# Queries and keys of an mLSTM layer projected token-major ahead of the values, and turned to features through VectorE and DRAM

## The chip, the cores and the metric

The program runs on one core of one Trainium2 chip. The metric is the device time of one execution in microseconds (us); for a kernel that was run several times it is the median of the runs. Beside the runs there is one execution taken by the hardware profiler, from which the page and the trace come; its span is counted from the first to the last instruction of the core.

The engines are named as in the profile: PE is TensorE with its matmuls, PEld its weight loads, DVE is VectorE, ACT is ScalarE, POOL is GpSimd and SP is SyncE, which here only issues DMAs. Each engine takes its instructions in a fixed order.

## The reference

The model is a decoder trunk of two layers over 256 tokens of width 2048, all in float32. The even layer joins a gated linear recurrence and a real-gated recurrent unit; the odd layer, which the change touches, is an mLSTM with eight heads (key width 128, value width 256) and an output gate. Each layer ends with a gated per-layer embedding. Cut to the odd layer:

```
hn = rmsnorm(h, o_norm)
u  = hn @ o_w_in            # 2048 -> 2048 (q,k) + 2048 (v) + 2048 (og) + 2048 (z) + 16 (gates)
qk = silu(causal_conv(u[qk], c_conv_w, c_conv_b))     # 4 taps along the tokens
li, lf = ig + c_b_i, log_sigmoid(fg + c_b_f)
yc = mlstm(q, k, v, li, lf)                            # stabilised, causal
yc = head_rmsnorm(yc, c_norm) * sigmoid(og) * silu(z)
h  = h + yc @ o_w_out
h  = h + sigmoid(h @ ple_gate_w) * rmsnorm(p @ ple_w, ple_norm)
```

The convolution runs along the tokens, for each of the 2048 query and key features by itself; the scores of the mLSTM need queries and keys with features on the partitions.

## The kernel before

**Products in three parts.** Every large product is made from float32 operands that are each split into a high part (`fp32r`) and a rest: high times high, high times rest, rest times high. `load_weights` (lines 119 to 134) does it for the weights: SP loads half a megabyte into a `raw` tile (line 128; five buffers), ACT casts it to `whi` (line 131) and DVE subtracts to get `wlo` (line 132); of `whi` and of `wlo` there are four buffers each, so a fifth tile can be cast only when PE has finished with the first. The activations are split the same way into tiles `ahl`.

**Two ways to project.** Token-major (`project_tok`, `quarter_tok`, lines 190 to 229): the activations are the stationary operand and the weights stream through, 512 columns at a time; one chunk of 512 output features takes four quarters of 24 matmuls (12 for the first 128 tokens, then 12 for the others), and the result has tokens on the partitions. Feature-major (`block`, lines 154 to 169): the weights are stationary and the activations stream; 128 output features take 16 matmuls of 512 columns (line 161: high weights with high and rest of the activations side by side) and 16 of 256 columns (line 167: rest of the weights), and the result has features on the partitions. `project` (line 176) joins two such blocks: ACT copies one half out (line 173), DVE adds the halves (line 174) and multiplies by the row norm (line 184). `chunks` (line 209) begins a stage with two chunks whose quarters are interleaved (line 203), since the activations of the last quarter arrive late.

**Lanes.** Longer side work is written as generators in named lanes (`start`, `step`, `drain`). `pump` (line 74) takes one step of each lane; it is called in the middle of each token-major quarter (line 229) and in the middle of each feature-major block (line 164). What a step issues is put behind the matmuls already recorded. The order of the instructions on each engine is then fixed by a scheduler that knows these orders, priorities and buffers.

**Turning tokens to features.** `to_features` and `feature_major` (lines 377 and 515) do it in three parts: DVE transposes the 32x32 squares of a 128x1024 tile into `w` (lines 382, 520); `across` (line 504) lets POOL write `w` to a DRAM tensor (line 507) and read it back with the squares in their new places into `r` (four DMAs, line 510); some pumps later ACT brings `r` into order while it applies a gain (lines 390, 527). `w` and `r` share four buffers (`room`, line 905). The kernel does this with the residual ahead of each gate product and with three quarters of the mLSTM's result.

**The odd layer.** Its stages on PE follow each other in this order: gate product of the even layer's embedding (`ple_gate`, line 932); values, token-major (line 970); queries and keys, feature-major, as 16 blocks in pairs (`qk_proj`, line 951): per pair of blocks ACT and DVE also run the convolution (line 958, then three taps per 128 features, line 961) and SiLU (tanh on ACT, line 964, and line 965 on DVE); output gate (line 1093) and gate z (line 1106), both token-major; the output product; the last gate product. The lane `mix` runs beside them: `gate_stats` (line 990) the input and forget gates, then `mix(j)` (line 1027) for two heads each: the stabilising weights (lines 265, 1034 to 1040), two pumps later the scores (lines 1047 to 1049), one pump later scores times values (lines 1059 to 1066). `mix(j)` is started when the queries and keys of its two heads are there. Tiles with the tag `vt` (six buffers) hold values, numerators and gates.

Of the kernel before, what the change touches and what calls it, by code (L numbers as in the profile page):

```python
# [11 lines left out]
F32 = mybir.dt.float32  # L12
# [3 lines left out]
AF = mybir.ActivationFunctionType  # L16
ALU = mybir.AluOpType
PSUM = bass.MemoryType.PSUM

P = 128  # L20
T = 256
# [22 lines left out]
def trunk(ctx: ExitStack, tc: tile.TileContext, a, out):  # L44
    nc = tc.nc
    v, s, gp, te, sy = nc.vector, nc.scalar, nc.gpsimd, nc.tensor, nc.sync
# [16 lines left out]
    def start(lane, gen):  # L63
        lanes.setdefault(lane, []).append(gen)
# [16 lines left out]
    def drain(*which):  # L81
        for lane in which:
            while step(lane):
                pass
# [26 lines left out]
    def pc(name, i=0, n=None):  # L111
        o, w = PRM[name]
        return prm[:, o + i:o + i + (n or 1)]
# [62 lines left out]
    def project(w, pair, act, which=(0, 1), rs=None):  # L176

        m = tp.tile([P, 512], F32, name="mg", tag="hn", bufs=3)
        for j in which:
            merge(m[:, j * T:(j + 1) * T], block(w[2 * pair + j], act))  # L180
        if rs is not None:
            n = len(which)
            m3 = m[:, which[0] * T:(which[0] + n) * T].rearrange("p (j t) -> p j t", j=n)
            v.tensor_tensor(out=m3, in0=m3, in1=rs.unsqueeze(1).to_broadcast([P, n, T]), op=ALU.mult)
        return m
# [275 lines left out]
    acth = []  # L461
# [28 lines left out]
    norm = {}  # L490
# [457 lines left out]
    with tc.tile_pool(name="m1", bufs=2) as m1:  # L948
        qk = {}

        def qk_proj(j):
            ps = project(a["oqk"], j, acth, rs=norm["rs"])
            d = m1.tile([P, 512], F32, name="qk", tag="qk", bufs=8)
            for i in range(2):
                b = 2 * j + i
                dst = d[:, i * T:(i + 1) * T]
                pi = ps[:, i * T:(i + 1) * T]
                s.activation(dst, pi, AF.Identity, scale=pc("ccw", 48 + b), bias=pc("ccb", b))  # L958
                for k in range(2, -1, -1):
                    sh = 3 - k  # L960
                    v.scalar_tensor_tensor(dst[:, sh:T], pi[:, 0:T - sh], pc("ccw", k * 16 + b), dst[:, sh:T],  # L961
                                           op0=ALU.mult, op1=ALU.add)
            th = tp.tile([P, 512], F32, name="th", tag="th")
            s.activation(th, d, AF.Tanh, scale=0.5)
            v.scalar_tensor_tensor(d, th, 1.0, d, op0=ALU.add, op1=ALU.mult)
            return d

        VW = 257
        vts = []
        for j, psv in enumerate(chunks(a["ov"], 4, acth, ready(acth, "fg"))):  # L970
            if j == 0:
                drain("norm")
            vt = m1.tile([P, 2, 2, VW], F32, name="vt", tag="vt", bufs=6)
            gp.memset(vt[:, :, :, 256:VW], 1.0)
            for hf in range(2):
                s.activation(vt[:, hf, :, 0:256], psv[hf].rearrange("p (i e) -> p i e", i=2), AF.Copy,
                             scale=norm["rt"][:, hf:hf + 1])
            vts.append(vt)
        gm = tp.tile([P, T], F32, name="sm", tag="sm")
        s.copy(gm, gps[:, 0:T])  # L980

# [88 lines left out]
        def mix_norm():  # L1070


            t, r, yh = (m1.tile([P, 16], F32, name=n, bufs=1) for n in ("nwt", "nwr", "nwy"))
            s.activation(den, den, AF.Abs)
            v.tensor_tensor(out=den, in0=den, in1=aT[:, 16:32], op=ALU.max)
            v.tensor_scalar(den, den, 1e21, EPS ** 0.5, op0=ALU.min, op1=ALU.mult)
            v.tensor_tensor(out=den, in0=den, in1=den, op=ALU.mult)
            v.scalar_tensor_tensor(den, ss, 1.0 / 256, den, op0=ALU.mult, op1=ALU.add)
            newton(den, t, r, yh)
            for hf in range(2):  # L1080
                c = slice(hf * 8, hf * 8 + 8)
                v.tensor_scalar(fac[:, c], r[:, c], norm["rt"][:, hf:hf + 1], 0.25, op0=ALU.mult, op1=ALU.mult)
            yield

        y = {}
        for j in range(4):
            qk[j] = qk_proj(j)
            qk[4 + j] = qk_proj(4 + j)
            start("mix", mix(j))
        start("mix", mix_norm())  # L1090
        held = []
        for j in range(4):
            ps = project_tok(a["oog"], j, acth)
# [179 lines left out]
def layout(x, p, e_norm, e_w_in, a_lb_logits, a_norm, b_conv_w, b_conv_b, b_w_r, b_b_r, b_w_i, b_b_i, b_lambda,  # L1273
# [4 lines left out]
    def put(name, arr):  # L1278
# [34 lines left out]
        "ez": _tm(za),  # L1313
        "bw": np.ascontiguousarray(bw.transpose(0, 3, 1, 2, 4).reshape(2, P, 2, 512)),
        "eo": _tm(wo),
        "oqk": _fm(ow[:, 0:2048]),
        "ov": _tm(ow[:, 2048:4096]),
        "oog": _tm(ow[:, 4096:6144]),
        "oz": _tm(ow[:, 6144:8192]),
# [23 lines left out]
```

## Time and profile before

| | |
|---|---|
| median of 3 runs | 1051.92 us (1051.46 to 1054.58) |
| profiled execution | 1052.27 us, its span 1050.2 us |
| granted TensorE clock | 0.998 |
| PE busy | 1040.0 us, 99% of the span |
| DVE, ACT, POOL busy | 729.0, 588.9, 105.5 us |
| last two value chunks | 527.5 to 571.1 us |
| queries and keys | 571.1 to 675.5 us |
| output gate, gate z | 675.5 to 762.8, 762.8 to 854.2 us |

The profiled execution is 0.35 us above the median of the runs, and 2.1 us longer than its span. In the trace a row of a timeline has the start, the length, the engine, the line and operation, the tiles as output<-input, their shape, and a count where equal rows are merged; the idle time of the engine just before it stands in brackets with what ended it. Matmuls overlap: one of 512 columns is shown with 0.39 us, but the next begins 0.23 us after it. So PE's work is read from starts, not from lengths.

### The profile page before, as it was taken

The numbers are of one execution on the slowest core, as the hardware profiler recorded it, in microseconds if no ns is written. First come the engines' busy times: TensorE is split into PE (matmuls) and PEld (weight loads), VectorE is DVE, ScalarE is ACT, GpSimd is POOL, SyncE is SP. The second block draws the span as 40 slices with busy tenths as digits, with TensorE's granted clock in tenths as the row PEclk, the third lists the DMA queues.
The fourth block names the chain that finished last, engine by engine and source line by source line (L and its number), as shares of the span: only waits on it lengthen the run. The fifth ranks groups of instructions, "written<-read, shape, count | busy, mean of one in ns | idle before, by whom it ended". The sixth has DMA issues, their size and how long they took to land.

```text
span 1050.2 us, 15196 instructions
## 1 busy us (share of the span) xinstructions
PE 1040.0 (99%) x5632; PEld 876.2 (83%) x5632; DVE 729.0 (69%) x1101; ACT 588.9 (56%) x885; POOL 105.5 (10%) x142
## 2 busy tenths in 40 slices
PE   9999999999999999999999999999999999999996
PEld 7888888888888888887888888888888888888886
DVE  6856897997877666766544887764457777666675
ACT  7775545869654444565544656654445565444553
POOL 0001332522201111111000000000001110111000
PEclk9999999999999999999999999999999999999999
DMA  9865454545867887687556544545557785877652
GB/s 356 302 209 196 166 168 155 181 156 194 273 234 247 264 242 235 207 276 225 188 191 200 173 154 156 170 161 197 197 189 222 249 269 185 291 244 241 201 181 81
DMA packets 63242, 221.21 MB, mean 211 GB/s; under 512 B 7744, under 2 KB 9024, under 8 KB 63168
## 3 DMA queue, kind: packets, MB, share of 16 engines
q1 hardware_dynamic: 55440, 196.38, 56.0%
q0 software_dynamic: 7152, 23.07, 7.2%
q8 instruction: 44, 0.72, 0.3%
q10 hardware_dynamic: 576, 0.79, 0.2%
q14 instruction: 30, 0.25, 0.1%
HBM read 209.20 MB, written 11.01 MB: 210 GB/s over the span
## 4 chain that ended last, share of the span: by engine, by line
PE 98%; DMA 1%; ACT 0%; SPq 0%; DVE 0%; issue 0%; ACTq 0%
PE mm L225 20%; PE mm L227 19%; PE mm L226 19%; PE mm L161 17%; PE mm L167 9%; PE mx L225 2%; PE mx L227 2%; PE mx L226 2%; PE mm L338 2%; PE mm L1178 1%; PE mm L1177 1%; PE mm L1176 1%; DMA raw<-in_pw_dram 1%; PE mx L823 1%; PE nu L1059 1%; PE mx L661 0%
## 5 line engine op out<-in xcount | busy, mean ns | idle before, releaser
L132 DVE TENSOR_TENSOR wlo<-raw,whi 128x1024 fp32r<-128x1024 f32 (+1 forms) x364 | 438.0, 1219 | 241.9 <-ACT whi L131 203.1
L131 ACT CAST whi<-raw 128x1024 fp32r<-128x1024 f32 (+1 forms) x364 | 378.0, 1042 | 354.8 <-PE mm L227 238.3
L225 PE MATMUL mm<-whi,ahl 128*128 128x512 f32 x896 | 350.3, 391 | 0.0
L227 PE MATMUL mm<-whi,ahl 128*128 128x512 f32 x896 | 348.6, 389 | 0.0
L226 PE MATMUL mm<-wlo,ahl 128*128 128x512 f32 x896 | 348.5, 389 | 0.0
L225 PEld LDWEIGHTS mm<-whi,ahl 128*128 128x128 f32 x896 | 168.2, 188 | 36.4 <-issue 1.6
L227 PEld LDWEIGHTS mm<-whi,ahl 128*128 128x128 f32 x896 | 168.2, 188 | 35.3
L226 PEld LDWEIGHTS mm<-wlo,ahl 128*128 128x128 f32 x896 | 168.2, 188 | 34.7 <-DVE wlo L132 0.2
L161 PE MATMUL mm<-ahl,whi 128*128 128x512 f32 x768 | 183.1, 390 | 0.0
L161 PEld LDWEIGHTS mm<-ahl,whi 128*128 128x128 f32 x768 | 141.3, 188 | 27.5
L167 PE MATMUL mm<-ahl,wlo 128*128 128x256 f32 x768 | 102.1, 286 | 0.0
L167 PEld LDWEIGHTS mm<-ahl,wlo 128*128 128x128 f32 x768 | 97.2, 191 | 3.6 <-issue 0.4
L225 PE MATMUL mx<-whi,ahl 128*128 128x512 f32 x96 | 37.5, 391 | 0.0
L227 PE MATMUL mx<-whi,ahl 128*128 128x512 f32 x96 | 37.4, 389 | 0.0
L226 PE MATMUL mx<-wlo,ahl 128*128 128x512 f32 x96 | 37.3, 389 | 0.0
L173 ACT COPY sm<-mm 128x256 f32<-128x256 f32 x48 | 17.6, 367 | 32.1 <-PE mm L167 31.9
L507 POOL DMA_DIRECT2D ducn<-w x3 | 1.7, 563 | 332.5 <-DVE w L520 332.5
L961 DVE SCALAR_TENSOR_TENSOR qk<-mg,prm,qk 128x255 f32<-128x255 f32 (+2 forms) x48 | 21.1, 477 | 5.0 <-ACT qk L958 4.7
L227 PEld LDWEIGHTS mx<-whi,ahl 128*128 128x128 f32 x96 | 18.0, 188 | 3.8
L226 PEld LDWEIGHTS mx<-wlo,ahl 128*128 128x128 f32 x96 | 18.0, 188 | 3.7
L225 PEld LDWEIGHTS mx<-whi,ahl 128*128 128x128 f32 x96 | 18.0, 188 | 3.7
L174 DVE TENSOR_TENSOR mg<-mm,sm 128x256 f32<-128x256 f32 x48 | 19.9, 415 | 0.1
(299 smaller groups left out, 862.1 us busy)
## 6 DMA issues: line engine op xcount, KB each, us to landing
raw<-in_ew_dram SPq DMA_DIRECT2D x64, 512.0 KB, 4.4
raw<-in_g_dram SPq DMA_DIRECT2D x56, 512.0 KB, 4.7
raw<-in_eo_dram SPq DMA_DIRECT2D x32, 512.0 KB, 5.0
raw<-in_ov_dram SPq DMA_DIRECT2D x32, 512.0 KB, 4.1
raw<-in_oqk_dram SPq DMA_DIRECT2D x32, 512.0 KB, 4.3
raw<-in_oog_dram SPq DMA_DIRECT2D x32, 512.0 KB, 3.9
raw<-in_oz_dram SPq DMA_DIRECT2D x32, 512.0 KB, 4.3
raw<-in_oo_dram SPq DMA_DIRECT2D x32, 512.0 KB, 4.5
```

Of the source, the lines that this page charges most:

```text
L131: last["act"] = s.copy(h, r).ins
L132: last["dve"] = v.tensor_tensor(out=l, in0=r, in1=h.bitcast(F32), op=ALU.subtract).ins
L161: last["pe"] = te.matmul(ps, parts[k // 8][0][:, c:c + P], act[k // 2][2][:, (k % 2) * 512:(k % 2 + 1) * 512], start=(k == 0), stop=False).ins
L167: last["pe"] = te.matmul(ps[:, T:2 * T], parts[k // 8][1][:, c:c + P], act[k // 2][0][:, k % 2], start=False, stop=(k == KT - 1)).ins
L173: s.copy(small, ps[:, T:2 * T])
L174: v.tensor_tensor(out=dst, in0=ps[:, 0:T], in1=small, op=ALU.add)
L225: te.matmul(ps[hf], xh, wh, start=(k == 0), stop=False)
L226: te.matmul(ps[hf], xh, wl, start=False, stop=False)
L227: last["pe"] = te.matmul(ps[hf], xl, wh, start=False, stop=(k == KT - 1)).ins
L338: last["pe"] = te.matmul(ps[hf], tokens(pact[x], k, hf), (hi, lo)[y][:, k * 512:(k + 1) * 512], start=(n == mine[0]), stop=(n == mine[-1]) ...
L823: te.matmul(ps[:, i * T:(i + 1) * T], bw[:, w, c * P:(c + 1) * P], xc[:, c * T:(c + 1) * T], start=True, stop=True)
L961: v.scalar_tensor_tensor(dst[:, sh:T], pi[:, 0:T - sh], pc("ccw", k * 16 + b), dst[:, sh:T], op0=ALU.mult, op1=ALU.add)
```

## The change

The weights of queries and keys are laid out for token-major products, and their stage is moved ahead of the values. It starts with the two interleaved chunks, as the values did. Each of its four chunks (512 features, tokens on the partitions) is copied out of PSUM by ACT with the row norm as its scale, into a tile `tqk` with the tag `vt`. A lane per chunk, `features`, transposes the squares, sends them through DRAM with the same `across` and its six pumps of delay, and then, for each pair of 128 features, lets ACT put the squares in order (a plain copy), and runs convolution and SiLU as before. The values follow as four plain chunks; after value chunk j the lanes of the features that heads 2j and 2j+1 need are drained and `mix(j)` is started. The feature-major blocks of this stage, their copies, sums and products with the norm are gone. Nothing else is edited.

```diff
-        def qk_proj(j):
-            ps = project(a["oqk"], j, acth, rs=norm["rs"])
-            d = m1.tile([P, 512], F32, name="qk", tag="qk", bufs=8)
...
+        def features(t, j):
+
+            w = room("w")
+            w5 = w.rearrange("p (j c h t) -> p h c j t", j=4, c=4, h=2)
+            for hf in range(2):
+                v.transpose(w5[:, hf], t[:, hf].rearrange("p (c j q) -> p c j q", c=4, j=4))
+            r = room("r")
+            yield from across(w, r, f"dqk{j}", 6)
+            r5 = r.rearrange("p (i c h t) -> p c h i t", i=4, c=4, h=2)
+            for b in range(2):
+                x = tp.tile([P, 512], F32, name="xr", tag="hn", bufs=3)
+                d = m1.tile([P, 512], F32, name="qk", tag="qk", bufs=8)
+                for i in range(2):
+                    n = 4 * j + 2 * b + i
+                    dst = d[:, i * T:(i + 1) * T]
+                    pi = x[:, i * T:(i + 1) * T]
+                    s.copy(pi.rearrange("p (h i t) -> p h i t", h=2, i=4), r5[:, 2 * b + i])
+                    s.activation(dst, pi, AF.Identity, scale=pc("ccw", 48 + n), bias=pc("ccb", n))
+                    for k in range(2, -1, -1):
+                        sh = 3 - k
+                        v.scalar_tensor_tensor(dst[:, sh:T], pi[:, 0:T - sh], pc("ccw", k * 16 + n), dst[:, sh:T],
+                                               op0=ALU.mult, op1=ALU.add)
+                th = tp.tile([P, 512], F32, name="th", tag="th")
+                s.activation(th, d, AF.Tanh, scale=0.5)
+                v.scalar_tensor_tensor(d, th, 1.0, d, op0=ALU.add, op1=ALU.mult)
+                qk[2 * j + b] = d
+                yield
+
+        for j, ps in enumerate(chunks(a["oqk"], 4, acth, ready(acth, "fg"))):
+            if j == 0:
+                drain("norm")
+            t = m1.tile([P, 2, 512], F32, name="tqk", tag="vt", bufs=6)
+            for hf in range(2):
+                s.activation(t[:, hf], ps[hf], AF.Copy, scale=norm["rt"][:, hf:hf + 1])
+            start(f"qk{j}", features(t, j))
+            step(f"qk{j}")
...
-        for j, psv in enumerate(chunks(a["ov"], 4, acth, ready(acth, "fg"))):
...
         for j in range(4):
-            qk[j] = qk_proj(j)
-            qk[4 + j] = qk_proj(4 + j)
+            psv = project_tok(a["ov"], j, acth)
+            vt = m1.tile([P, 2, 2, VW], F32, name="vt", tag="vt", bufs=6)
+            gp.memset(vt[:, :, :, 256:VW], 1.0)
+            for hf in range(2):
+                s.activation(vt[:, hf, :, 0:256], psv[hf].rearrange("p (i e) -> p i e", i=2), AF.Copy,
+                             scale=norm["rt"][:, hf:hf + 1])
+            vts.append(vt)
+            for c in (j // 2, 2 + j // 2):
+                drain(f"qk{c}")
             start("mix", mix(j))
...
-        "oqk": _fm(ow[:, 0:2048]),
+        "oqk": _tm(ow[:, 0:2048]),
```

**PE, at the scores of two heads.** In the kernel before, the four matmuls of the scores of `mix(1)` stand between the two halves of a feature-major block:

```order
L161 MATMUL mm<-ahl,whi 128x512 x16
L1047 MATMUL mx<-qk 128x256
L1048 MATMUL mx<-qk 128x128
L1047 MATMUL mx<-qk 128x256
L1048 MATMUL mx<-qk 128x128
L167 MATMUL mm<-ahl,wlo 128x256 x16
```

After the change the scores (now lines 1058 and 1059) stand in the middle of a token-major quarter of the values, first those of `mix(0)` in the third quarter of the second value chunk:

```order
L226 MATMUL mm<-wlo,ahl 128x512
L227 MATMUL mm<-whi,ahl 128x512
L1058 MATMUL mx<-qk 128x256
L1059 MATMUL mx<-qk 128x128
L1058 MATMUL mx<-qk 128x256
L1059 MATMUL mx<-qk 128x128
L225 MATMUL mm<-whi,ahl 128x512
```

What moved: rows of lines 161 and 167 no longer stand in this stage, and the side matmuls, the same in number, are set into rows of lines 225 to 227.

**DVE, where convolutions stand between the splits of weights.** Before, in the stage of queries and keys (`mg` is the joined pair of blocks, `sm` the half that ACT copied, `scw` the weighted scores):

```order
L174 TENSOR_TENSOR mg<-mm,sm 128x256
L965 SCALAR_TENSOR_TENSOR qk<-th,qk 128x512
L132 TENSOR_TENSOR wlo<-raw,whi 128x1024 x2
L174 TENSOR_TENSOR mg<-mm,sm 128x256
L184 TENSOR_TENSOR mg<-mg,hrs 128x512
L961 SCALAR_TENSOR_TENSOR qk<-mg,prm,qk 128x255
L961 SCALAR_TENSOR_TENSOR qk<-mg,prm,qk 128x254
L961 SCALAR_TENSOR_TENSOR qk<-mg,prm,qk 128x255
```

After it, in the fourth chunk of queries and keys, from the second split for its second quarter on (`xr` is a pair of feature tiles brought back from DRAM):

```order
L132 TENSOR_TENSOR wlo<-raw,whi 128x1024
L956 STREAM_TRANSPOSE w<-tqk 128x4x4x32
L971 SCALAR_TENSOR_TENSOR qk<-xr,prm,qk 128x255 x2
L971 SCALAR_TENSOR_TENSOR qk<-xr,prm,qk 128x254 x2
L971 SCALAR_TENSOR_TENSOR qk<-xr,prm,qk 128x253 x2
L132 TENSOR_TENSOR wlo<-raw,whi 128x1024 x2
L975 SCALAR_TENSOR_TENSOR qk<-th,qk 128x512
L971 SCALAR_TENSOR_TENSOR qk<-xr,prm,qk 128x255 x2
L971 SCALAR_TENSOR_TENSOR qk<-xr,prm,qk 128x254 x2
L971 SCALAR_TENSOR_TENSOR qk<-xr,prm,qk 128x253 x2
L132 TENSOR_TENSOR wlo<-raw,whi 128x1024 x2
L975 SCALAR_TENSOR_TENSOR qk<-th,qk 128x512
```

What moved: the sums of line 174 and products of line 184 are gone, transposes of line 956 have come, and the taps of the first two chunks, which end a quarter apart, now stand in one run, six before every two splits of weights.

More of the change, by code (lines that the diff above doesn't have):

```diff
@@ L949, in trunk @@
         qk = {}
-        def qk_proj(j):
-            ps = project(a["oqk"], j, acth, rs=norm["rs"])
-            d = m1.tile([P, 512], F32, name="qk", tag="qk", bufs=8)
[L954 to L966, printed above, removed]
+        def features(t, j):
[24 more added lines that the diff above has]
+                yield
@@ L968, in trunk @@
+        for j, ps in enumerate(chunks(a["oqk"], 4, acth, ready(acth, "fg"))):
[6 more added lines that the diff above has]
+            step(f"qk{j}")
         VW = 257
         vts = []
-        for j, psv in enumerate(chunks(a["ov"], 4, acth, ready(acth, "fg"))):
[L971 to L978, printed above, removed]
@@ L1083, in mix_norm @@
             yield
-        y = {}
         for j in range(4):
-            qk[j] = qk_proj(j)
-            qk[4 + j] = qk_proj(4 + j)
+            psv = project_tok(a["ov"], j, acth)
[7 more added lines that the diff above has]
+                drain(f"qk{c}")
             start("mix", mix(j))
         start("mix", mix_norm())
+        y = {}
         held = []
```

## The prediction

> **What bounds the kernel now.** I read the page's busy times first, then the table of waits for PE.
>
> ```profile
> PE 1040.0 (99%) x5632; PEld 876.2 (83%) x5632; DVE 729.0 (69%) x1101; ACT 588.9 (56%) x885; POOL 105.5 (10%) x142
> ```
> ```profile
> PE st L95 <- POOL ones L90: 1.1, 1, 1.1
> PE mm L338 <- DVE wlo L132: 0.4, 1, 0.4
> ```
>
> PE is busy for 99% of the span, and the whole table of its waits (us in total, times, longest) holds two rows, 1.5 us, both at the start. So the kernel is a queue of matmuls, and a change is worth what it takes off that queue, less the waits that it brings. Waits could come from DVE and ACT, which split each weight tile. A table by stage shows their load: the gate product with the first two value chunks; the last two value chunks; queries and keys. Its columns are the stretch and its length, busy time of PE, PEld, DVE, ACT and POOL, the granted clock, the DMA share and GB/s.
>
> ```profile
> 418.00:527.50 109.50, 109.50 (x502) 88.33 (x502) 70.25 (x95) 62.71 (x92) 11.20 (x24) 1.00 0.72 227
> 527.50:571.10 43.60, 43.60 (x194) 36.09 (x193) 19.67 (x17) 19.43 (x20) 0.00 (x0) 1.00 0.58 193
> 571.10:675.50 104.40, 104.40 (x590) 90.84 (x589) 81.89 (x141) 66.04 (x121) 0.00 (x0) 1.00 0.51 167
> ```
>
> DVE has 0.78 of the query-and-key stage and 0.45 of the value chunks ahead of it. The clock is granted in full throughout, so durations can be carried from one stage to another.
>
> **Part 1: 16 feature-major blocks become four token-major chunks.** The chain shows a block as 16 matmuls of line 161 and 16 of line 167; PE's timeline in the value stage shows the starts of two matmuls that are 96, one chunk, apart.
>
> ```profile
> 583.13 3.65 PE mm L161 x16
> 586.78 1.91 PE mm L167 x16
> 588.69 3.65 PE mm L161 x16
> ```
> ```profile
> 527.59 0.39 PE L225 MATMUL mm<-whi,ahl 128*128 128x512 f32 x1
> ...
> 549.35 0.39 PE L225 MATMUL mm<-whi,ahl 128*128 128x512 f32 x1
> ```
>
> A block lasts 588.69 - 583.13 = 5.56 us, 16 of them 88.96 us. A chunk lasts 549.35 - 527.59 = 21.76 us (0.2267 per matmul), four of them 87.04 us. The difference is **-1.92 us**. It comes from the 256-column matmuls: 1.91/16 = 0.119 us each, more than half of the 0.228 of a 512-column one.
>
> The Trainium skill ("TensorE: Matmul & The Clock Gate", section "Back-to-back issue gap") states 518 cycles for 512 columns and 262 for 256 at 2.4 GHz; by these figures a block would be an estimated 5.20 us, a chunk 20.72, and the gain 0.3 us. The rows are 5% and 9% above the page's figures, and they decide.
>
> **Part 2: the side matmuls are set into another stream.** Their number is the same. One whole `mix` in feature-major surroundings lies in four blocks of the chain; one in token-major surroundings lies in the eight chunks of the output gate and gate z.
>
> ```profile
> 622.05 3.65 PE mm L161 x16
> ...
> 648.84 3.65 PE mm L161 x16
> ```
> ```profile
> 675.48 0.40 PE L225 MATMUL mm<-whi,ahl 128*128 128x512 f32 x1
> ...
> 854.25 0.39 PE L338 MATMUL mm<-whi,ahl 128*128 128x512 f32 x1
> ```
>
> The first costs 26.79 - 4 x 5.56 = 4.55 us, the second 178.77 - 8 x 21.76 = 4.69. Three `mix` change surroundings (the fourth had token-major ones already): 3 x 0.14 = **+0.4 us**. The gate sums (lines 993 and 1017) change too and have no row in token-major surroundings; I take 0 for them, since the scores' restarts cost alike in both. From below the term is 0, from above I double it: +0.8.
>
> **Part 3: DVE and ACT.** By the rows of single operations (busy, mean ns, then idle time before), of DVE in the query-and-key stage and of ACT in the odd layer's first half:
>
> ```profile
> L132 DVE TENSOR_TENSOR wlo<-raw,whi 128x1024 fp32r<-128x1024 f32 x32 | 37.8, 1220 | 6.7 <-ACT whi L131 2.9 <-issue 2.8 <-PE mm L167 0.8
> L961 DVE SCALAR_TENSOR_TENSOR qk<-mg,prm,qk 128x254 f32<-128x254 f32 x14 | 6.6, 480 | 0.2
> ...
> L174 DVE TENSOR_TENSOR mg<-mm,sm 128x256 f32<-128x256 f32 x15 | 6.2, 417 | 0.1
> L184 DVE TENSOR_TENSOR mg<-mg,hrs 128x512 f32<-128x512 f32 x7 | 4.8, 692 | 0.2
> L965 DVE SCALAR_TENSOR_TENSOR qk<-th,qk 128x512 f32<-128x512 f32 x7 | 4.8, 689 | 1.3 <-ACT th L964 1.3
> ```
> ```profile
> L390 ACT ACTIVATE xr<-r,prm 128x256 f32<-128x256 f32 x16 | 7.2, 501 | 0.0
> ...
> L173 ACT COPY sm<-mm 128x256 f32<-128x256 f32 x16 | 5.9, 366 | 13.0 <-PE mm L167 13.0
> ...
> L964 ACT ACTIVATE th<-qk 128x512 f32<-128x512 f32 x8 | 5.0, 626 | 3.1 <-DVE qk L961 3.1
> ```
> ```profile
> 436.06 0.70 DVE L382 STREAM_TRANSPOSE w<-hq 128x512 f32<-128x512 f32 x1
> 436.69 0.71 DVE L434 SCALAR_TENSOR_TENSOR hq<-th,rp,hq 128x512 f32<-128x512 f32 x1
> 437.32 2.35 DVE L132 TENSOR_TENSOR wlo<-raw,whi 128x1024 fp32r<-128x1024 f32 x2
> ```
>
> DVE loses 16 sums and 8 products, 6.7 + 5.5 = 12.2 us, and gains 8 transposes of 0.70, 5.6. ACT loses 16 copies, 5.9 us, and gains 16 copies of `xr` (the trace has no plain copy of this view: between 0.37 as line 173 and 0.50 as line 390, which reads the same view; I take 0.50) and 8 copies of 512 columns (about 0.63 as line 964): +7.1 us net. DVE then has 95 of these 148 us, 0.64. What matters is one crowd: chunks 1 and 2 of the stage end one quarter apart, and the taps and SiLU rows of both fall into the four quarters of the fourth chunk, as the rows in the part on the change show. How early a split is done, the value stage shows:
>
> ```profile
> 532.95 2.59 DVE L132 TENSOR_TENSOR wlo<-raw,whi 128x1024 fp32r<-128x1024 f32 x2 [2.85 <-ACT whi L131]
> ```
> ```profile
> 538.47 0.39 PE L225 MATMUL mm<-whi,ahl 128*128 128x512 f32 x1
> ```
>
> That pair of splits is for the quarter that begins at 538.47: the first is done at 532.95 + 1.22 = 534.17, and the second matmul needs it at 538.7. That is **4.5 us of cover**; with four buffers there can't be more, since the cast waits for PE to free the tile. Now the crowd, by the rate at which DVE takes such rows in a queue:
>
> ```profile
> 602.85 2.45 DVE L961 SCALAR_TENSOR_TENSOR qk<-mg,prm,qk 128x255 f32<-128x255 f32 x6
> ```
>
> Six taps end 2.45 us after the first began; less the last one's 0.48 that is 1.97 for five starts, 0.40 each. A transpose occupies the queue for 436.69 - 436.06 = 0.63, a 512-wide row 437.32 - 436.69 = 0.63, a split 2.35 - 1.22 = 1.13. The fourth chunk has 24 taps, 4 SiLU rows, 2 transposes and 8 splits: 9.6 + 2.5 + 1.3 + 9.0 = 22.4 us, in 21.76: 0.7 too much. A SiLU row also waits for a tanh of 0.63 that starts after the last tap; one or two splits stand between, of 1.13 each, so I let 0.2 show, 0.8 for four. About 3 us of the cover are left, PE doesn't wait, and the part costs **0**. Its bound from above is the first rival.
>
> **Part 4: the trip through DRAM, and the queues passed.** The same trip runs twice in a row in the gate product, behind the transpose at 436.06:
>
> ```profile
> 437.06 0.56 POOL L507 DMA_DIRECT2D dfg<-w  x1 [31.25 <-DVE w L382]
> 441.06 2.19 POOL L510 DMA_DIRECT2D r<-dfg  x4 [3.43 <-DMA dfg<-w]
> 443.24 0.56 POOL L507 DMA_DIRECT2D dfg<-w  x1
> 451.37 2.19 POOL L510 DMA_DIRECT2D r<-dfg  x4 [7.57 <-issue]
> ```
> ```profile
> DMA to landing us min/median/max: 3.2/6.0/7.6
> ```
>
> The first takes at most 443.25 + 7.6 - 436.06 = 14.8 us, the second, which waits longer for a place, 453.56 + 7.6 - 443.24 = 17.9 from its issue, some 19 in all. After the change the first chunk is complete one quarter before the third begins, and about 3 us later it is transposed (two casts and two splits stand ahead). On ACT's queue the first copy of its `r` stands behind a cast that waits for PE to finish the third quarter of the third chunk, 16.3 us into it. So the trip has 16.3 + 2.4 = 18.7 us before it could hold up anything, and 4.5 of cover. POOL's four trips are 4 x 2.75 = 11 us on an engine that is idle there; the value memsets now stand among them, behind trips that end quarters before. The transfers add 2 MB written and 2 MB read where the DMA share is 0.51 to 0.58; at 0.72 the gate product makes the same trips beside the same weight loads and PE waits for none. SP's load of `praw` (line 313) moves up among the weight loads and is half of one. This all costs 0; without its cover, what the trip takes beyond 23.2 us.
>
> **Sum.** -1.92 + 0.42 = -1.5 us. Against the profiled execution: 1052.27 - 1.5 = 1050.8. That execution lies 0.35 above the median of the runs, 1051.92; on their scale the forecast is **1050.4 us**.
>
> **Rivals.** (1) *The crowd on DVE makes PE wait: slower.* If DVE begins a row only when the one before has ended, the fourth chunk asks for 24 x 0.48 + 4 x 0.69 + 2 x 0.70 + 8 x 1.22 = 25.4 us, and with four tanh in full 27.9: 6.1 over. With the cover whole, PE waits 1.6; with the cover spent before, by the transposes that wait for the end of a chunk, all 6.1. I take the middle, 3.9: 1054.3, with 6.1 it is 1056.5. It decides, against the gain, from 6.0 us over with the cover whole. The row of six taps speaks against it: 2.45 us, where six in full are 2.88. The Trainium skill ("VectorE: DVE Perf Modes", section "The DRAIN you can't avoid") states it as a rule: the next operation does not start until the pipe is empty. The trace does not agree: 0.40 from start to start where one lasts 0.48.
> (2) *The trip lands late.* If it takes twice the 14.8 us, the first is 29.6 - 23.2 = 6.4 us over: 1056.8. Against it speak all eight trips of the two products with such trips before, which no PE wait names.
> (3) *The gain is larger.* The query-and-key stage has 104.40 - 88.96 = 15.4 us of side matmuls with their restarts; if the new stream took a sixth off them, 2.6 us, it would be 1050.0 - 2.6 = 1047.4 (part 2 at 0). The two sums of part 2, alike within 3%, speak against it.
>
> **Chances.** Forecast 0.78, with a range of its own from 1049.8 to 1051.4 (part 2 at 0 or doubled, and the scatter of medians); rival 1 0.13, a third of it above 1055.1; rival 2 0.04; rival 3 0.05. About 0.3%, 3.2 us, is what a measurement of this kernel can tell from no change: faster is below 1048.8, slower above 1055.1. So faster 0.05, same 0.87, slower 0.08. The range holds the forecast and the lighter half of rival 1: 1049.2 to 1053.8.
>
> **What would show it.** In the profile after: four chunks of 21.8 us each ahead of the values; from the first matmul of the first of the two stages to the first of the output gate 1.5 us less than before; PE's table of waits with its two rows and none on `wlo` or `whi` from the fourth chunk on; six taps in 2.45 us; ACT waiting at line 967 for no DMA. PE waiting for `wlo` in the fourth chunk would show rival 1, a wait of ACT at the copies of `xr` rival 2. The forecast is wrong if PE waits somewhere, or if a token-major chunk is slower beside the taps than beside plain splits.

## The result, and the profile after

The kernel after takes **1050.47 us** (median of 21 runs, 1050.06 to 1051.17), the kernel before beside it 1051.82 (21 runs, 1051.46 to 1054.58). The ratio is 0.9987, with a 95% interval of 0.9981 to 0.9992: a gain of 1.35 us by the medians, 0.8 to 2.0 by the interval. The profiled execution of after took 1051.14 us, its span 1049.4, against 1052.27 and 1050.2 before.

The page's busy times of the kernel after, and its table of what PE waited for (us in total, times, longest):

```profile
PE 1038.6 (99%) x5504; PEld 869.1 (83%) x5504; DVE 724.3 (69%) x1085; ACT 594.3 (57%) x893; POOL 114.4 (11%) x162
```
```profile
PE st L95 <- POOL ones L90: 1.1, 1, 1.1
PE mm L338 <- DVE wlo L132: 0.6, 1, 0.6
```

PE has 128 matmuls fewer, as 16 blocks of 32 against four chunks of 96 give, and waits at the same two places as before. Where the time went is read from three side matmuls in the chain of work that ended last (start, length): the first gate sum (line 929), the second part of `mix(3)`'s spread in the output gate (line 265), and the embedding's second half (line 338). First the kernel before:

```profile
466.96 0.57 PE mx L929 x8
...
678.39 0.43 PE mx L265 x2
...
854.41 5.45 PE mm L338 x24
...
860.30 5.50 PE mm L338 x24
```

The same three in the kernel after:

```profile
467.26 0.57 PE mx L929 x8
...
677.09 0.43 PE mx L265 x2
...
853.12 5.62 PE mm L338 x24
...
859.19 5.50 PE mm L338 x24
```

The two touched stages lie between the first and the second: 678.39 - 466.96 = 211.43 us before, 677.09 - 467.26 = 209.83 after, **1.60 us less**. From there to the last row it is 181.91 before and 182.10 after; of these 0.19, 0.17 are in the row of 5.62 against 5.45. In it one weight load of this execution waits 0.28 us for ACT (line 349). The row is 5.45 again in the profiled executions without the scores, with half of the taps doubled and with a shorter lag (below), so the 0.17 belong to this execution and not to the change. Both waits of PE's table lie elsewhere, in the first 13 us of the span. Outside the touched stages the execution of after is the longer one, by 0.30 us up to the first gate sum, 0.19 to the last row and 0.3 to its end, which is why the spans differ by 0.8 and not by 1.60.

The load by stage, as in the prediction: the gate product with the first two query-and-key chunks, the last two such chunks, and the values. The columns are the stretch and its length, busy time of PE, PEld, DVE, ACT and POOL, granted clock, DMA share, GB/s.

```profile
418.30:527.88 109.58, 109.58 (x503) 88.39 (x502) 71.66 (x98) 62.80 (x92) 11.52 (x21) 1.00 0.73 226
527.88:571.40 43.52, 43.52 (x193) 36.04 (x192) 34.07 (x50) 27.70 (x40) 7.77 (x15) 1.00 0.87 264
571.40:674.20 102.80, 102.80 (x461) 84.18 (x460) 65.37 (x101) 64.06 (x115) 3.00 (x8) 1.00 0.55 181
```

DVE has 34.07 of 43.52 us in the last two query-and-key chunks; the last two value chunks, which stood at that place before, had 19.67 of 43.60. The DMA share there rose from 0.58 to 0.87. Two chunks in 43.52 us are 21.76 each: a token-major chunk is no slower beside the taps. The clock is granted in full. The crowd of the fourth chunk, in DVE's timeline (start, length, line, tiles, count of rows merged):

```profile
553.36 2.47 DVE L971 SCALAR_TENSOR_TENSOR qk<-xr,prm,qk 128x255 f32<-128x255 f32 x6
555.74 2.36 DVE L132 TENSOR_TENSOR wlo<-raw,whi 128x1024 fp32r<-128x1024 f32 x2
558.01 0.69 DVE L975 SCALAR_TENSOR_TENSOR qk<-th,qk 128x512 f32<-128x512 f32 x1
558.62 2.46 DVE L971 SCALAR_TENSOR_TENSOR qk<-xr,prm,qk 128x255 f32<-128x255 f32 x6
```

Six taps take 2.46 to 2.47 us, a pair of splits 2.36, and no row stands with idle time ahead of it: the crowd is there as forecast. The trip's end, in ACT's timeline:

```profile
545.37 0.70 ACT L967 COPY xr<-r 128x256 f32<-128x256 f32 x2
```

The copies of `xr` (0.40 us each in the mean of 16, less than the 0.50 of the prediction) show no wait for a DMA, neither these first two nor the others.

### The profile page after: what moved, and what is told of

The parts are those of the page before. It is cut to its first block, busy times and chain, and to the rows that moved or that the text cites. A ratio compares the mean times of both kernels' runs of the same rounds, so it can differ in the third digit from the quotient of the medians.

```text
span 1049.4 us, 14961 instructions
## 1 busy us (share of the span) xinstructions
PE 1038.6 (99%) x5504; PEld 869.1 (83%) x5504; DVE 724.3 (69%) x1085; ACT 594.3 (57%) x893; POOL 114.4 (11%) x162
## 4 chain that ended last, share of the span: by engine, by line
PE 97%; DMA 1%; ACT 1%; DVE 0%; issue 0%; SPq 0%; ACTq 0%
PE mm L225 22%; PE mm L226 22%; PE mm L227 22%; PE mm L161 11%; PE mm L167 6%; PE mx L225 2%; PE mx L227 2%; PE mx L226 2%; PE mm L338 1%; DMA xq<-in_xT_dram 1%; PE mm L1196 1%; PE mm L1195 1%; PE mm L1194 1%; PE mx L823 1%; PE nu L1070 1%; PE mx L661 0%
## 5 line engine op out<-in xcount | busy, mean ns | idle before, releaser
L225 PE MATMUL mm<-whi,ahl 128*128 128x512 f32 x1024 | 401.5, 392 | 0.0
L227 PE MATMUL mm<-whi,ahl 128*128 128x512 f32 x1024 | 398.5, 389 | 0.0
L226 PE MATMUL mm<-wlo,ahl 128*128 128x512 f32 x1024 | 398.4, 389 | 0.0
L225 PEld LDWEIGHTS mm<-whi,ahl 128*128 128x128 f32 x1024 | 192.2, 188 | 42.0 <-issue 2.1
L227 PEld LDWEIGHTS mm<-whi,ahl 128*128 128x128 f32 x1024 | 192.2, 188 | 40.5
L226 PEld LDWEIGHTS mm<-wlo,ahl 128*128 128x128 f32 x1024 | 192.3, 188 | 39.8 <-DVE wlo L132 0.5
L161 PE MATMUL mm<-ahl,whi 128*128 128x512 f32 x512 | 122.1, 390 | 0.0
L161 PEld LDWEIGHTS mm<-ahl,whi 128*128 128x128 f32 x512 | 94.2, 188 | 18.3
L167 PE MATMUL mm<-ahl,wlo 128*128 128x256 f32 x512 | 67.7, 285 | 0.0
L167 PEld LDWEIGHTS mm<-ahl,wlo 128*128 128x128 f32 x512 | 64.9, 191 | 2.2
L971 DVE SCALAR_TENSOR_TENSOR qk<-xr,prm,qk 128x255 f32<-128x255 f32 (+2 forms) x48 | 20.4, 475 | 0.6 <-ACT qk L968 0.5
L1195 PE MATMUL mm<-wlo,ahl 128*128 128x256 f32 x64 | 18.1, 283 | 0.0
```

The lines of the kernel that those rows point to most:

```text
L161: last["pe"] = te.matmul(ps, parts[k // 8][0][:, c:c + P], act[k // 2][2][:, (k % 2) * 512:(k % 2 + 1) * 512], start=(k == 0), stop=False).ins
L167: last["pe"] = te.matmul(ps[:, T:2 * T], parts[k // 8][1][:, c:c + P], act[k // 2][0][:, k % 2], start=False, stop=(k == KT - 1)).ins
L225: te.matmul(ps[hf], xh, wh, start=(k == 0), stop=False)
L226: te.matmul(ps[hf], xh, wl, start=False, stop=False)
L227: last["pe"] = te.matmul(ps[hf], xl, wh, start=False, stop=(k == KT - 1)).ins
L1195: te.matmul(ps[hf], xh, wl, start=False, stop=False)
```

## The experiments

Line numbers in an experiment's rows are its own; they are named with what stands there.

**Scores left out, before and after: parts 1 and 2 apart.** In both kernels the body of `mix` from its spreads to its squares is replaced by copies of the values; the part left out is the scores, their weights, their products with the values, and the denominators and squares taken from these:

```diff
         def mix(j):
...
-            ps = px.tile([P, 512], F32, name="mx", tag="mx")
...
             nm = m1.tile([P, 2, 512], F32, name="num", tag="vt", bufs=6)
...
-                    s.activation(sq, ps[:, 0:256], AF.Square, accum_out=ss[:, c:c + 1])
+            for hf in range(2):
+                s.copy(nm[:, hf].rearrange("p (i e) -> p i e", i=2), vts[j][:, hf, :, 0:256])
...
```

> The kernel before, without the scores and their products (all of mix but the copies into num, which are made from the values instead), so that the matmul stream of the two stages is free of side matmuls but for the gate sums and gate statistics. Its time is read only against the same cut of the kernel after: by the two prices of a mix it is 3 x 4.55 + 4.69 = 18.3 us below the kernel before, 1033.6.

> The kernel after with the same part left out (the scores and their products). My theory: with no mix, part 2 of the prediction falls away and the whole of part 1 shows: from the first gate sum to the first matmul of the output gate it is 1.92 us shorter than the kernel before with the same cut, and the mix in token-major surroundings costs 0.1 more apiece than in feature-major ones, so the kernel is 18.7 us below after: 1031.8. If the layout itself were worth only the 1.5 to 1.6 us that the full kernels show, that stretch is 1.5 to 1.6 shorter and part 2 is 0. If the interplay of scores and blocks was worth something (rival 3), the stretch differs by under 1 us.

Measured: 1033.61 us (4 runs, 1033.22 to 1034.28) and 1031.91 (5 runs, 1031.47 to 1034.74); ratios to before 0.9826 (0.9813 to 0.9840) and 0.9817 (0.9803 to 0.9830). Both are within 0.15 us of the forecasts, but the runs scatter too much to part 1.9 from 1.6; the chain of work does that. The first gate sum and the embedding's second half in the kernel before without scores, then in the kernel after without them:

```profile
466.28 0.57 PE mx L929 x8
...
841.55 5.50 PE mm L338 x24
```
```profile
466.66 0.57 PE mx L929 x8
...
839.97 5.50 PE mm L338 x24
```

841.55 - 466.28 = 375.27 us against 839.97 - 466.66 = 373.31: the layout alone is worth **1.96 us**. With the scores the same stretch is 860.30 - 466.96 = 393.34 before and 859.19 - 467.26 = 391.93 after. So four `mix` cost 393.34 - 375.27 = 18.07 us before, and after it 391.93 - 373.31 = 18.62, of which 0.17 is the longer row at the embedding: 18.45, or **0.38 us more**. Each stretch is from one execution; how well such a stretch repeats, the run with a lag of 5 quarters (below) shows, where the layout and the order of the scores are those of the kernel after: 860.58 - 468.83 = 391.75 us, against 391.93 less 0.17. The theory holds in both parts; that the layout is worth 1.6 and the scores cost alike falls, and so does a gain from their interplay.

**Taps issued again: how much cover the crowd has.** A tap is followed by one of the same shape into a scratch tile, in the run with half of the taps for every other 128 features, as shown; in the run with all of them the line with `if` is left out.

```diff
...
                         v.scalar_tensor_tensor(dst[:, sh:T], pi[:, 0:T - sh], pc("ccw", k * 16 + n), dst[:, sh:T],
                                                op0=ALU.mult, op1=ALU.add)
+                        if i == 0:
+                            v.scalar_tensor_tensor(extra[:, sh:T], pi[:, 0:T - sh], pc("ccw", k * 16 + n),
+                                                   pi[:, sh:T], op0=ALU.mult, op1=ALU.add)
```

> Half of the taps (12 of the 24 in the fourth query-and-key chunk) are issued a second time, into a scratch tile that nobody reads; the outputs are the same. My theory: the crowd in the fourth chunk grows by 12 x 0.40 = 4.8 us, of which the cover that is left, 3.7 us in the profile after, takes 3.7; PE waits about 1.1 us on wlo (0.5 to 2.5), time about 1051.6. If DVE began a row only when the one before has ended (rival 1), the extra rows are 12 x 0.48 = 5.8 us and the cover was mostly gone before: PE waits 3.3 to 5.8 us, time 1053.8 to 1056.3. If the cover is much larger than I count, PE waits for nothing and the time is 1050.5.

> All 24 taps are issued a second time, into a scratch tile that nobody reads; the outputs are the same. My theory: 24 x 0.40 = 9.6 us more in the fourth chunk, less 3.7 of cover: PE waits about 5.9 us on wlo there, time about 1056.4; the first value chunk then asks DVE for about 21.8 us in 21.76 and brings no cover back, so up to 2 us more may come behind it: 1055.5 to 1058.5. Against the run with half of the taps doubled the slope is 1: 4.8 us more taps, 4.8 us more time. Rival 1: 11.5 us more rows and little cover, PE waits 9 to 11.5, time 1059.5 to 1062. If the cover is much larger than I count, the wait is below 4 us.

Measured: with half of the taps doubled 1050.96 us (10 runs, 1050.39 to 1051.31; ratio 0.9990, 0.9981 to 0.9999), with all of them 1061.62 (4 runs, 1060.41 to 1064.86; ratio 1.0096, 1.0079 to 1.0114). The first costs less than forecast, the second more, so the slope isn't 1, and the table of waits has no row for `wlo` in either. PE's timeline in the run with all taps doubled shows where it waits: the last gate sum (line 929), the gate statistics' first matmul (line 1008), the first of their last two groups (line 1032), the products of the first scores with the values (line 1074).

```profile
518.20 0.64 PE L929 MATMUL mx<-r,wg 128*32 128x256 f32 x8
...
578.84 0.62 PE L1008 MATMUL mx<-sm,cst 128*40 128x256 f32 x2
...
606.45 0.61 PE L1032 MATMUL mx<-cst,li 8*128 8x8 f32 x4 [2.73 <-DVE li L1020]
...
631.66 2.05 PE L1074 MATMUL nu<-vt,scw 128*128 128x257 f32 x4 [3.29 <-DVE scw L1064]
```

The first two of these rows in the kernel after, where the gate statistics stand at line 1004:

```profile
519.02 0.64 PE L929 MATMUL mx<-r,wg 128*32 128x256 f32 x8
...
579.66 0.62 PE L1004 MATMUL mx<-sm,cst 128*40 128x256 f32 x2
```

From the one to the other, with the whole crowd between them, it is 60.64 us in both. So 9.6 us more work for DVE in the fourth chunk cost PE nothing there. My theory, that the crowd's excess is paid out of the splits' cover, falls. In the order that the scheduler made for this kernel the splits of each quarter stand between the taps in DVE's queue, so a backlog is one of taps, and it ran on into the values. There it reached the statistics in two ways. Their first row on DVE came 12.8 us later than in the kernel after, counted from the last gate sum (592.40 there, 580.45 in the kernel after). The last transpose of the fourth chunk came 9.5 us later (582.54, 573.88), so its trip landed late, ACT stood for it just ahead of the statistics' own rows, and DVE stood for ACT:

```profile
597.73 0.71 ACT L969 COPY xr<-r 128x256 f32<-128x256 f32 x2 [2.65 <-DMA r<-dqk]
```
```profile
600.22 0.28 DVE L1016 TENSOR_SCALAR ab<-ab 8x256 f32<-8x256 f32 x1 [2.52 <-ACT ab L1015]
```

At the second wait it is the taps alone: twelve of them, doubles included, stand without a gap on DVE from 626.24 us to 631.05, and then comes the weighting of the scores (line 1064) for which PE waits.

The waits sum to 2.73 + 3.29 = 6.02 us, but from the first gate sum to the scores of `mix(3)` (in the chain 466.44 to 697.65, in the kernel after 467.26 to 688.64) the run is 231.21 - 221.38 = 9.83 us longer. The rest is in the granted clock, the first column behind POOL's in this table of the stretches behind the two waits:

```profile
604.00:608.00 4.00, 1.55 (x7) 1.39 (x8) 4.00 (x7) 2.43 (x6) 0.00 (x0) 0.93 0.66 228
608.00:612.00 4.00, 4.00 (x14) 2.97 (x14) 3.79 (x8) 2.87 (x4) 0.00 (x0) 0.65 0.54 146
612.00:616.00 4.00, 4.00 (x20) 3.11 (x21) 2.17 (x7) 0.42 (x1) 0.00 (x0) 1.00 0.59 190
629.00:632.00 3.00, 0.34 (x1) 0.37 (x2) 3.00 (x8) 0.63 (x1) 0.00 (x0) 0.88 0.00 0
632.00:636.00 4.00, 4.00 (x13) 2.97 (x12) 1.66 (x6) 2.52 (x9) 0.00 (x0) 0.66 0.00 0
636.00:640.00 4.00, 4.00 (x19) 3.27 (x19) 1.96 (x4) 3.87 (x10) 0.10 (x1) 1.00 0.00 0
```

The time lost to the clock is the length of a stretch times the share that is not granted: 4 x 0.07 + 4 x 0.35 = 1.7 us behind the first wait and 3 x 0.12 + 4 x 0.34 = 1.7 behind the second; 6.02 + 3.4 = 9.4 of the 9.83. In the run with half of the taps PE waits for nothing in these stages, and the 0.56 us by which it is longer (676.83 - 466.44 = 210.39 against 209.83, from the first gate sum to the spread of `mix(3)`) arises behind the statistics' first matmul, which again stands 60.64 us behind the last gate sum. There the statistics' last two groups and the first spread, one row of side matmuls in the kernel after (596.77 to 597.75), stand at three places (595.94, 597.84, 599.51).

**All taps doubled, the side chain four quarters later.** The test of the new theory: `mix` begins later, all else as in the run with all taps doubled.

```diff
         def gate_stats():
             yield
+            for _ in range(4):
+                yield
```

> All taps issued twice, as before, into a scratch tile that nobody reads, and the gate statistics with the scores behind them begin four quarters later; the outputs are the same. New theory, from the profile of the run with all taps doubled: the splits stand between the taps in DVE's queue, so a backlog there is one of taps, and PE waited only where a side matmul needs what comes behind the taps (2.7 us for the gate statistics, 3.3 for the first score). With four quarters more, 21.8 us, for that chain, both waits go, and the time falls from 1061.6 to 1050.5 to 1053. If it were the amount of DVE work itself that cost PE its 11 us, the time stays near 1061.6.

Measured: 1052.89 us (10 runs, 1051.37 to 1056.68; ratio 1.0011, 1.0001 to 1.0021), inside the forecast. Of the two waits, which were both to go, one is left, at the same matmuls of the statistics; here the clock behind it stays full:

```profile
PE mx L1034 <- DVE li L1022: 1.8, 1, 1.8
```
```profile
622.00:626.00 4.00, 2.23 (x12) 1.58 (x10) 4.00 (x8) 1.39 (x2) 0.00 (x0) 1.00 0.31 100
626.00:630.00 4.00, 4.00 (x19) 3.00 (x19) 3.77 (x10) 2.66 (x4) 0.00 (x0) 1.00 0.58 208
```

Of the 11.15 us that the doubled taps cost over the kernel after, 8.73 go with the order of the side chain alone, at the same work for DVE. What cost PE most of its time was the chain behind the taps, not the amount of DVE work.

**A shorter lag: how long the trip takes.** With 5 quarters, as shown, and with 4:

```diff
-            yield from across(w, r, f"dqk{j}", 6)
+            yield from across(w, r, f"dqk{j}", 5)
```

> The lag between the trip through DRAM and the copies of xr is 5 quarters in place of 6, so ACT comes to the first copy about 5.4 us earlier, at about 540. The trip's last landing is bounded to 543.0 in the profile after. My theory: ACT waits for the DMA by 0 to 3.1 us, the cover of 4.5 us takes it, PE waits for nothing: 1050.5, within 0.5. If the trip takes twice what I counted (rival 2), ACT waits over 10 us and the time is above 1056.

> The lag is 4 quarters: ACT comes to the first copy about 10.9 us earlier than after the change, at about 534.5. My theory: the first trip takes the 14.8 us of the prediction, from the transpose at 524.9 to 539.7, so ACT waits 5.2 us for its DMA, cover takes 4.5, PE waits 0.7 us (0 to 4, the upper end if the landing is as late as 543.0); time 1051.2, from 1050.5 to 1054.5. Rival 2 (the trip takes twice that): ACT waits over 15 us and PE over 10, time above 1060.

Measured: 1051.44 us with 5 (10 runs, 1050.14 to 1052.96; ratio 0.9993, 0.9983 to 1.0003) and 1055.64 with 4 (6 runs, 1053.88 to 1056.92; ratio 1.0032, 1.0020 to 1.0044). With 5, ACT stands 3.6 us in all at the copies (four waits, the longest 2.05), and PE waits for nothing in these stages; the stretch from the first gate sum to `mix(3)`'s spread is 678.66 - 468.83 = 209.83 us, that of the kernel after to 0.01. The median is still 0.4 us above the forecast of 1050.5 within 0.5. The profiled execution (1052.54) is longer for waits of 1.5 us in the first embedding, ahead of the touched stages; what the others of the ten above 1051 us waited for isn't shown. With 4, the transpose on DVE that completes the first chunk, and the first copies on ACT:

```profile
524.59 0.70 DVE L956 STREAM_TRANSPOSE w<-tqk 128x512 f32<-128x512 f32 x1
```
```profile
539.57 0.71 ACT L967 COPY xr<-r 128x256 f32<-128x256 f32 x2 [5.28 <-DMA r<-dqk]
```

ACT stands at the copy 5.28 us and the data is there at 539.57: the trip takes **15.0 us** from the transpose, where at most 14.8 was forecast, and the wait was forecast at 5.2. Cover took it: the statistics' first matmul is at 579.37, 60.64 us behind the last gate sum at 518.73. What the forecast missed comes later. ACT waits 13.6 us for the four trips together, the fourth time ahead of the last exponential of the gate statistics (line 1019), and PE waits for that:

```profile
PE mx L1028 <- ACT Bc L1019: 1.2, 1, 1.2
```
```profile
595.00:599.00 4.00, 2.81 (x16) 2.02 (x15) 3.72 (x10) 3.97 (x7) 0.00 (x0) 1.00 0.61 196
599.00:603.00 4.00, 4.00 (x11) 3.06 (x12) 3.44 (x5) 3.31 (x6) 0.00 (x0) 0.58 0.28 78
603.00:607.00 4.00, 4.00 (x19) 3.27 (x18) 3.97 (x9) 3.59 (x6) 0.00 (x0) 0.99 0.54 188
```

A wait of 1.2 us and 4 x 0.42 = 1.7 us of lost clock behind it are about what this execution's span is longer (1052.1 against 1049.4). The median of 1055.64 is above the whole range of the forecast (1050.5 to 1054.5): the other five executions took longer than the profiled one, up to 1056.92 against 1053.88, and what they waited for isn't shown.

**The order without the layout.** The 16 feature-major blocks of before, moved ahead of the values:

```diff
+        for kq in range(4):
+            ready(acth, "fg")(kq)
+        drain("norm")
+        for j in range(8):
+            qk[j] = qk_proj(j)
...
-        for j, psv in enumerate(chunks(a["ov"], 4, acth, ready(acth, "fg"))):
...
+        for j, psv in enumerate((project_tok(a["ov"], j, acth) for j in range(4))):
...
-            qk[j] = qk_proj(j)
-            qk[4 + j] = qk_proj(4 + j)
```

> The order without the layout: the kernel before with its 16 feature-major query-and-key blocks put ahead of the values; nothing is left out. A feature-major block needs all 16 activation tiles in its first 16 matmuls. In the profile after, the stage begins at about 480 and the last of those tiles is split at 508.3 to 510.1, about 20 us after its trip could begin. My theory: PE runs 12 matmuls and then waits 18 to 26 us for the last quarter of the activation: time 1070 to 1078. If order alone were free, it is 1051.9 as before, and the layout's share is then the whole gain.

Measured: 1064.28 us, one execution, beside 1052.01 for the kernel before: it is slower by 12 us, less than the 18 to 26 forecast. PE's table of waits, and the table by stretches behind:

```profile
PE mm L161 <- DVE ahl L146: 6.6, 1, 6.6
```
```profile
491.00:495.00 4.00, 0.69 (x4) 0.23 (x2) 0.00 (x0) 0.37 (x1) 2.27 (x6) 0.91 0.44 131
495.00:499.00 4.00, 0.73 (x2) 0.50 (x2) 1.11 (x2) 2.84 (x6) 0.00 (x0) 0.50 0.00 0
499.00:503.00 4.00, 4.00 (x23) 1.75 (x22) 0.27 (x1) 1.04 (x1) 0.00 (x0) 0.50 0.00 0
503.00:507.00 4.00, 4.00 (x26) 3.83 (x26) 2.54 (x3) 1.51 (x3) 0.00 (x0) 0.81 0.12 23
```

Two things were off. PE runs 36 matmuls of line 161 before it needs the last activation, three times the 12 that I counted. And that activation came sooner (the wait ends at 498.3, not at 508): ACT stood only for the DMA ahead of its last copies, at 495.68, where in the kernel after it comes to them at 506.49, behind casts of weights. Of the 12 us, 6.6 are the wait, 4 x 0.50 + 4 x 0.19 = 2.8 clock lost behind it, and 2.0 two smaller waits (0.9 and 1.1); about 0.9 is not placed. The sign is as forecast: order alone is a loss. In the kernel after the stage stands first without such a wait; its interleaved token-major quarters take the activations piece by piece.

**The same step once more, in the even layer.** The kernel after with the input of the even layer's recurrence token-major too: 2 chunks for 8 blocks, with transposes, `across` and convolution as in `features`. Two more runs issue the reads one quarter behind the write, with a lag of 4 and of 3 quarters in all:

```diff
...
-        start("rg", rg_lru(0, xb_proj(0)))
-        start("rg", rg_lru(1, xb_proj(1)))
+        for r in range(2):
+            ps = project_tok(a["exb"], r, acth)
+            t = hp.tile([P, 2, 512], F32, name="txb", tag="h")
+            for hf in range(2):
+                s.activation(t[:, hf], ps[hf], AF.Copy, scale=norm["rt"][:, hf:hf + 1])
+            start(f"rg{r}", xb_features(r, t))
+            step(f"rg{r}")
...
```

> The same step applied once more, on top of the change: the 8 feature-major blocks of the input of the linear recurrence in the even layer become 2 token-major chunks, brought to features through DVE's transposes and DRAM with a lag of 4 quarters; nothing is left out. My theory: the blocks give 2 x 21.76 - 8 x 5.56 = -0.96 us and, if DVE and ACT keep up beside the attention of the same stage, the time is 1049.5. Rival: DVE is fuller there than in the query-and-key stage, the transposes and the later convolution delay splits or the recurrence, and PE waits by more than 1 us: 1050.5 to 1060.

> As the run with the even layer's blocks made token-major, but each trip's reads are issued one quarter after its write, so that POOL takes its attention products in between; the lag in all stays 4 quarters. Theory: there PE waited 4.0 us behind POOL, which stood 5.7 us for the landing of the write, and had half the clock for some 4 us after it, about 6 us in all; with that wait gone, the time is 1050 to 1052.5. If the wait only moves (to the second product behind the reads, or to the later convolution), it is 1053 to 1057.5.

> The same with a lag of 3 quarters in all, so that the convolution begins 5.4 us earlier. Theory: as the run with 4, and the wait of 1.4 us on the gate product's sum at 296 goes as well: 1049.5 to 1051. If ACT comes to the copies before the trip has landed (15 us from the transposes, against 16.3 that 3 quarters give), PE waits by 0 to 3 us more than with 4.

Measured: 1057.45 us (5 runs, 1056.79 to 1057.95; ratio 1.0051, 1.0039 to 1.0064), 1058.58 (4 runs, 1057.38 to 1059.46; 1.0063, 1.0046 to 1.0080) and 1059.03 (4 runs, 1057.31 to 1059.81; 1.0062, 1.0047 to 1.0077). All three are slower than both kernels. In the first, POOL's timeline shows the trip's write, its reads after 5.66 us of standing, and only then a product of the attention, for which PE waits:

```profile
212.67 0.60 POOL L507 DMA_DIRECT2D dxb<-wx  x1 [8.64 <-DVE wx L804]
218.93 2.19 POOL L510 DMA_DIRECT2D rx<-dxb  x4 [5.66 <-DMA dxb<-wx]
...
222.91 1.05 POOL L740 TENSOR_TENSOR k<-k,tot 128x512 f32<-128x512 f32 x1
```
```profile
224.01 1.08 PE L733 MATMUL mx<-f,k 128*32 128x32 f32 x64 [4.05 <-POOL k L740]
```

With the reads put later that wait falls to 0.9 us, but the time doesn't fall. PE's waits in the run with a lag of 4:

```profile
PE mm L161 <- DVE mg L174: 2.6, 1, 2.6
PE mm L226 <- DVE wlo L132: 1.5, 2, 1.2
PE mx L842 <- ACT av L846: 1.5, 1, 1.5
...
PE mx L733 <- POOL k L740: 0.9, 1, 0.9
```

My theory that the queue behind POOL was the whole cost falls: the waits in that stage sum to 6.5 us, where the first run had 4.0 and 1.4, and are spread over splits, the recurrence and the gate product. With a lag of 3 the wait for POOL is gone, and others sum to 5.9 us (2.8 for the recurrence, 1.7 for splits, 1.4 for a cast). The stage carries the attention as well, and with none of the three lags is it free of waits. Whether another order would be is open.

## Why the prediction was right

- **The bound.** PE's queue was the bound and stayed it: 99% busy, the same two waits at the start.
- **Part 1, -1.92 us.** Measured -1.96, with the scores left out.
- **Part 2, +0.42 us.** Measured +0.38. The sum of both, -1.5, is -1.60 in the touched stages of the profiled executions and -1.35 on the medians. The interval of the gain, 0.8 to 2.0 us, is wide beside these terms: that the median came out within 0.07 us of the forecast is luck in part, and it is the stretches of the chain that bear out the two terms.
- **Part 3, 0.** The number is right: PE waits nowhere in the crowd. Some reasons for it were not. The copies of `xr` take 0.40 us, not 0.50, and ACT's load grew by 5.4 us in place of 7.1; DVE has 99.4 us in the two stages in place of 95. Neither matters here. But the step "about 3 us of the cover are left" named the wrong limit: 9.6 us more of taps in that chunk don't delay a split that PE needs. In the fourth chunk the taps give way, not the splits, and what is at risk is what stands behind the taps in DVE's queue: the transposes of the fourth chunk, the gate statistics and the scores of the values' stage. With 4.8 us more no wait showed there, with 9.6 two.
- **Part 4, 0.** Right in size as well: the trip takes 15.0 us from the transpose in the run with a lag of 4 (at most 14.8 forecast), and ACT comes to the first copy at 545.37, 20.5 us behind the transposes at 524.88, where I had counted 18.7. So 5.5 us are left ahead of the cover, about one quarter; with a lag of 5 the touched stages of the profiled execution take the same 209.83 us.
- **Rival 1, the crowd makes PE wait.** It didn't, and the place was wrong. Its ground, that a row begins only when the one before has ended, is refuted by six taps in 2.46 us. The prediction read the Trainium skill too narrowly there ("VectorE: DVE Perf Modes", section "The DRAIN you can't avoid"): the section goes on that a next operation that is not held starts earlier, and the trace agrees with that (0.40 us from start to start where one lasts 0.48). Rival 1's price was too low as well: I priced a wait of PE by its length, and a wait of 2.7 us cost 4.4 here. The Trainium skill has this ("TensorE: Matmul & The Clock Gate", section "What's actually happening": the array's clock goes to half after an idle window of about 3.4 us, and the window runs freely). The trace agrees with the half clock (0.50 from 608 to 610 us with all taps doubled), but it also fell to half behind a wait of 1.2 us, and stayed full behind one of 2.8.
- **Rival 2, the trip lands late.** Refuted by the 15.0 us, and in the kernel after by copies that wait for no DMA. **Rival 3, a larger gain.** Refuted by 18.07 against 18.45 us for the four `mix`.

## What to carry to other kernels

When an engine in a fixed order gets more work than fits, ask what stands behind the new work in its queue and who waits for that: here the splits were safe between the taps, and the small statistics at the end of the row were not. Price a stall of PE by its length and, if the trace shows it, by the clock behind it. A gain of 2 us by arithmetic is kept only while the trip behind it has time: with a lag of 4 quarters in place of 6 it was gone (1055.64 us), and in the even layer the same step, worth 1 us by arithmetic, lost 7 to 9.

## What the hardware showed that I had not expected

- **The clock behind a wait of PE.** In 4 us behind waits of 2.73, 3.29 and 1.19 us the granted clock was 0.65, 0.66 and 0.58 in the mean, with 0.50 in the lowest microseconds; it was 1.00 behind waits of 1.77 us (doubled taps, side chain later), 2.6 us (even layer, lag 4) and 2.8 us (even layer, lag 3). So the length of a single wait doesn't decide it; what does is not settled here.
- **A trip's write holds the queue that issues the read.** POOL stood 2.7 to 7.1 us between a write of half a megabyte to DRAM and its reads wherever the timeline of a profiled execution names that DMA as the reason, and what stood behind it in that queue, as the product of the attention above, stood too.
